# Mixers' loads on GpSimd's queue, a staging buffer of its own for the modulation, and split weights in four places of 128 columns

## The chip, the core and the metric

The kernel runs on one core of a Trainium2 chip. The metric is the device time of one execution in microseconds, the median of several runs. The core has a tensor engine for matrix products (PE), a vector engine (DVE), a scalar engine for activations (ACT), a general engine (GpSimd, called POOL in the profile) and an engine that only synchronises and starts transfers (SP). Each engine works through its own list of instructions in order. Transfers (DMAs) are started by an instruction in the list of SP, ACT or POOL: such an instruction waits for its semaphores there, and all that stands behind it in that list waits with it.

## What is computed

A model of two layers works on two streams of tokens, the latent `l` (512 tokens) and the context `c` (256 tokens), with 1024 channels, in float32:

```python
for i in range(DEPTH):                       # 2 layers
    m_l = split(silu(c)     @ mod_w[i] + mod_b[i], 6)   # modulation: shift, scale, gate, twice
    m_c = split(silu(c_ctx) @ mod_w[i] + mod_b[i], 6)
    ul = split_cols(modulate(rms_norm(h_l), m_l[0], m_l[1]) @ w_in[i])   # 1024 x 2696
    uc = split_cols(modulate(rms_norm(h_c), m_c[0], m_c[1]) @ w_in[i])
    y_l = concat(ssd(ul, uc), hyena(ul), retention(ul, uc), s5(ul, uc)) @ w_out[i]
    h_l = h_l + m_l[2] * y_l
    h_l = h_l + m_l[5] * swiglu(modulate(rms_norm(h_l), m_l[3], m_l[4]), w_up[i], w_down[i])
    ...                                      # the same for the context, in the first layer alone
return rms_norm(h_l)
```

Four mixers share the columns of the input projection: SSD (a scan with 4 heads), Hyena (long convolutions by spectra, whose filters are made by a small network), retention (a scan with 4 heads and a rotary table) and S5 (a complex diagonal state space with 16 groups).

## The kernel before

**Products.** A float32 matrix product is made of three products of float32r parts (`mm3`, matmuls at L126). A weight comes as pieces of 128 columns by 1024 rows (512 KB): `piece` (L207) loads one into the staging tile `wst`, which has three buffers, on SP's queue; `split` makes the high part `whi` on ACT (L155) and the low part `wlo` on DVE (L134); `weights` collects two pieces into one pair of tiles `whi`, `wlo` of 256 columns, of which there are two in turn (pool `whl`, two buffers each). `held` (L227) does the same for the output projection's second half. `dt_weights` takes a whole pair for 128 columns (`wd`, L1125), and block `sb` a pair for one piece.

**Modulation of the first layer.** `mod` makes 256 columns at a time: two loads of 512 KB (each four of the eight row tiles) through the same `wst` buffers, 16 matmuls `wst,csil` with 32 rows of output into one PSUM bank (ring `md`, one bank), a copy by ACT (`mrow`), two small matmuls `const,mrow` and an addition on DVE (`modv`). Eight such blocks stand in `start`, twelve more among blocks 5 to 10 of the input projection (`in_proj`). The second layer's modulation and a last eighth of the first's are products on DVE (`mod_vec`, L361, loads `mvw` on POOL's queue).

**Order of the work.** A scheduler writes each engine's list at build time from priorities (`at`, `flow`) and a simulated timeline. The big projections carry `bulk` (their priority is pushed back by 300000), so that the mixers' small products go first and the projections fill in. PSUM banks come from rings: `mm` (3 banks) for the projections, `xb` (2) and `xa` (2) for the mixers, `md` (1). In the first layer ring `xb` makes the Hyena filters of the context and of the latent stream (`sirens`, `filters`), then the convolutions of the context, then those of the latent stream; ring `xa` makes the S5 blocks (`s5_mats` with `s5_block`, eight blocks of two groups), then `s5_out`, then SSD; retention follows in `mm` and `xa`. The output projection begins after them.

**Small loads of the mixers.** Before, SP's list holds besides the weights: the rotary table (L1645), in the first layer the filters' small weights and tables (L504 to L540: `w`, `feat`, `win`) and their spectra's stores (L598: `F0`), the SSD's and retention's decay rows (`E` L897, `CE` L964, `scanm` L1156), and S5's rotations (`s5rot` L1466), kernels (`KT` L1471, read from what ACT's queue wrote as `s5k`), inputs (`s5U` L1473) and the loads of `s5_out` (`s5fu` L1535, `s5fy` L1537), and the mixers' outputs that are read back (`yl` L1714). POOL's list holds the filters' Fourier tables (`ftab`, L581), in the second layer all that the filters load, and some element-wise work (`fam`, `aloc`, `alol`, `t`, and the mask on `E`, L719).

Of the kernel before, what the change touches and what calls it, by code (L numbers as in the profile page):

```python
# [17 lines left out]
D = 1024  # L18
# [88 lines left out]
class Kern:  # L107
# [7 lines left out]
    def at(self, p):  # L115
        """Instructions in this block get priorities from p on."""
# [44 lines left out]
    def pst(self):  # L161
        """A PSUM bank from the ring of the current flow of work."""
# [13 lines left out]
    def flow(self, fl, p=None):  # L176
        """Work that takes its banks and small tiles from rings of its own; p: its priority."""
# [10 lines left out]
    def rsq(self, v, n):  # L188
        """v: (128, n) tile, replaced by 1/sqrt(v)."""
# [13 lines left out]
    def piece(self, src, nk, ncol):  # L203
        """src: (128, nk * ncol) of a weight laid out by pieces."""
        pool, tag = self.stage
        st = pool.tile([128, 1024], F32, tag=tag, name="wst", bufs=2 if tag == "stw" else 3)[:, :nk * ncol]
        self.nc.sync.dma_start(st, src)  # L207
        return st.rearrange("p (k n) -> p k n", k=nk)

    def weights(self, srcs, nk=8):  # L210
        """Pieces of 128 columns as high and low parts."""
        hi = self.whl.tile([128, 8, 256], F32R, tag="wh", name="whi")
        lo = self.whl.tile([128, 8, 256], F32R, tag="wl", name="wlo")
        for h, src in enumerate(srcs):
            cs = slice(128 * h, 128 * h + 128)
            self.split(hi[:, :nk, cs], lo[:, :nk, cs], self.piece(src, nk, 128))
        return hi, lo

    def held(self, src):
        """Four tiles of rows of a weight with all its columns, src: (8, 128, 512)."""  # L220
        W = []
        for m0 in (0, 4):
            hi = self.whl.tile([128, 8, 256], F32R, tag="wh", name="whi").rearrange("p k n -> p (k n)")
            lo = self.whl.tile([128, 8, 256], F32R, tag="wl", name="wlo").rearrange("p k n -> p (k n)")
            for h in range(2):
                st = self.wst.tile([128, 1024], F32, tag="st", name="wst")
                self.nc.sync.dma_start(st.rearrange("p (m x) -> p m x", m=2),  # L227
                                       src[m0 + 2 * h:m0 + 2 * h + 2].rearrange("m p x -> p m x"))
                self.split(hi[:, 1024 * h:1024 * h + 1024], lo[:, 1024 * h:1024 * h + 1024], st)
            W += [[t[:, 512 * m:512 * m + 512].rearrange("p (k n) -> p k n", k=4) for t in (hi, lo)] for m in range(4)]  # L230
        return W

    def proj(self, ps, W, c0, m, a, nk=8, order=None):
        hi, lo = W
        ah, al = a
        with self.bulk():
            for q, k in enumerate(order or range(nk)):
                self.mm3(ps, hi[:, k, c0:c0 + m], lo[:, k, c0:c0 + m], ah[k], al[k], q == 0, q == nk - 1)
# [14 lines left out]
    def run(self):  # L253
        nc, tc, A = self.nc, self.tc, self.A
        es = ExitStack()
        with es:
# [4 lines left out]
            self.whl = ec(tc.tile_pool(name="whl", bufs=2))  # L261
# [15 lines left out]
    def put_y(self, s, k, t, c0=0):  # L277
        """Keep tile k of the mixers' output: as operands of the output projection where these have room already."""
# [12 lines left out]
    def ytiles(self, s, p):  # L291
        """Tiles that are not written in the order of their making: each has its own place."""
# [41 lines left out]
    def mod(self, i, c0, c1):  # L334
        """Columns 256*c0 .. 256*c1 of the modulation of layer i."""
        for cc in range(c0, c1):
            with self.flow("md"):
                ps = self.pst()
            for h in range(2):
# [3 lines left out]
            r = self.tile_t(self.sc, "mrow")  # L343
            self.act(r, ps[:, :256])
            p2 = ps[:, 256:260]
            for h in range(2):
                self.mm(p2[:, 2 * h:2 * h + 2], r[:, 128 * h:128 * h + 128], self.sel[:, 3:5])
            self.add(self.modv[i][:, 2 * cc:2 * cc + 2, :], p2.rearrange("p (a b) -> p a b", a=2),
                     self.vec[i][:, 2 * cc:2 * cc + 2][:, :, None].to_broadcast([128, 2, 2]))
# [20 lines left out]
    def gains(self, i, part, s, gat):  # L370
        """(1 + scale) * g for a stream; part is 1 or 4."""
# [1531 lines left out]
```

## Time and profile before

| what | us |
|---|---|
| median of three runs | 1916.04 (1914.66 to 1916.39) |
| span of the profiled execution | 1919.5 |
| PE busy in it | 1790.1 |
| DVE busy | 1257.5 |
| ACT busy | 713.5 |
| POOL busy | 207.3 |

The profiled execution's own time is its span, 1919.5 us, from the first instruction to the last; it lies 3.5 us above the median of the runs. Busy times are of instructions that compute; the issue of transfers from SP isn't counted. The mean granted clock of PE was 0.960 of its full 2.4 GHz. In the page's slices the clock reads full in most of the span, and lower where PE had gaps: in the first layer's mixers (0 to 520 us), in the second layer's (1180 to 1560) and at the end.

### The profile page before, as it was taken

To read this page: it belongs to the slowest core of one execution; us is meant where nothing else is said; L and a number is where in the kernel's file an instruction comes from. 1 tells how busy PE (TensorE), PEld (TensorE's weight loads), DVE (VectorE), ACT (ScalarE), POOL (GpSimd) and SP (SyncE) were. 2 spreads that over 40 slices of the span, in tenths; PEclk is the share of its full clock that TensorE was granted. 3 is DMA by queue.
4 is the path that set the end of the run, shared out by engine and by line. 5 is a ranking of instruction groups with operands and counts; after the bars stand their busy time and mean duration, and the time that the engine had idled before them with its cause. 6 is when DMAs were issued, how large, how long until landed. Compare 5 with 4: busy or idle time off the path is not lost.

```text
span 1919.5 us, 28992 instructions
## 1 busy us (share of the span) xinstructions
PE 1790.1 (93%) x10792; PEld 1526.3 (80%) x10792; DVE 1257.5 (66%) x2941; ACT 713.5 (37%) x1390; POOL 207.3 (11%) x273
## 2 busy tenths in 40 slices
PE   3789878898999999999999999989999999999997
PEld 2678767686789888888888989878866888888886
DVE  8788764778858899777665427678576843233336
ACT  4354234555227223212132115514673542222222
POOL 0201121123002000011223000121110000000000
PEclk9899979998899999999999999999997999999998
DMA  6656588765612335656635513565563322222331
GB/s 231 178 138 186 149 180 229 243 192 160 203 56 89 121 123 164 219 190 230 210 113 131 155 44 123 158 207 159 153 201 96 126 73 94 89 96 88 97 101 56
DMA packets 193089, 280.87 MB, mean 146 GB/s; under 512 B 51745, under 2 KB 127837, under 8 KB 192436
## 3 DMA queue, kind: packets, MB, share of 16 engines
q1 hardware_dynamic: 107188, 166.20, 28.5%
q10 hardware_dynamic: 55920, 64.72, 10.9%
q0 software_dynamic: 29840, 48.09, 8.9%
q8 instruction: 85, 1.39, 0.3%
q14 instruction: 56, 0.46, 0.1%
HBM read 235.00 MB, written 43.96 MB: 145 GB/s over the span
## 4 chain that ended last, share of the span: by engine, by line
PE 58%; DVE 11%; issue 8%; DMA 8%; ACT 3%; POOL 1%; ACTq 0%; SPq 0%; DVEq 0%; POOLq 0%
PE ps_mm L126 31%; PE ps_xb L126 20%; PE ps_xa L126 4%; DMA mvw<-in_wmt_dram 4%; PE ps_md L126 2%; DMA wst<-in_wi_dram 1%; ACT L155 1%; DVE mvo L364 1%; DVE wlo L134 1%; DVE gt L134 1%; DVE t L134 1%; DVE g L1499 1%; DVE cst L134 1%; DVE s5tmp L134 1%; ACT whi L155 1%
## 5 line engine op out<-in xcount | busy, mean ns | idle before, releaser
L155 ACT ACTIVATE whi<-wst 128x1024 fp32r<-128x1024 f32 (+3 forms) x226 | 198.9, 917 | 361.5 <-PE ps_mm L126 169.4
L134 DVE TENSOR_TENSOR wlo<-wst,whi 128x1024 fp32r<-128x1024 f32 (+3 forms) x226 | 233.9, 1058 | 83.5 <-ACT whi L155 81.2
L126 PE MATMUL ps_mm<-alol,whi 128*128 128x512 f32 (+1 forms) x688 | 262.7, 383 | 0.4 <-POOL alol L134 0.4
L126 PE MATMUL ps_mm<-ahl,wlo 128*128 128x512 f32 (+1 forms) x688 | 262.3, 382 | 0.0
L126 PE MATMUL ps_mm<-ahl,whi 128*128 128x512 f32 (+1 forms) x688 | 260.9, 383 | 0.3 <-ACT ahl L155 0.2
L126 PE MATMUL ps_mm<-h,whi 128*128 128x512 f32 (+1 forms) x592 | 168.8, 365 | 0.9 <-DVE h L134 0.7
L126 PE MATMUL ps_xb<-ahl,whi 128*128 128x512 f32 (+1 forms) x416 | 154.2, 373 | 3.8 <-ACT ahl L155 3.8
L126 PE MATMUL ps_xb<-ahl,wlo 128*128 128x512 f32 (+1 forms) x416 | 153.8, 370 | 0.0
L126 PE MATMUL ps_xb<-alol,whi 128*128 128x512 f32 (+1 forms) x416 | 153.5, 371 | 0.1
L134 DVE TENSOR_TENSOR sg<-sg,ps_mm 128x512 f32<-128x512 f32 (+1 forms) x70 | 39.9, 570 | 172.9 <-PE ps_mm L126 172.7
L126 PEld LDWEIGHTS ps_mm<-alol,whi 128*128 128x128 f32 x688 | 130.7, 190 | 26.4 <-issue 2.7
L126 PEld LDWEIGHTS ps_mm<-ahl,wlo 128*128 128x128 f32 x688 | 130.7, 190 | 24.5 <-issue 1.1
L126 PEld LDWEIGHTS ps_mm<-ahl,whi 128*128 128x128 f32 x688 | 130.2, 191 | 25.0 <-issue 1.6
L126 PE MATMUL ps_xb<-h,whi 128*128 128x256 f32 (+1 forms) x592 | 129.2, 310 | 0.1
L364 DVE SCALAR_TENSOR_TENSOR mvo<-mvw,crow 128x1024 f32<-128x1024 f32 x80 | 97.8, 1222 | 39.6 <-DMA mvw<-in_wmt_dram 38.7
L126 PE MATMUL ps_mm<-ahc,whi 128*128 128x256 f32 x368 | 107.4, 296 | 13.0 <-ACT whi L155 8.6
L126 PEld LDWEIGHTS ps_mm<-h,whi 128*128 128x128 f32 x592 | 103.7, 188 | 17.5 <-DVE h L134 1.2
L126 PE MATMUL ps_mm<-aloc,whi 128*128 128x256 f32 x368 | 108.2, 295 | 1.0 <-DVE aloc L134 1.0
L126 PE MATMUL ps_mm<-ahc,wlo 128*128 128x256 f32 x368 | 107.1, 293 | 2.0 <-DVE wlo L134 2.0
L126 PEld LDWEIGHTS ps_xb<-h,whi 128*128 128x128 f32 x592 | 98.9, 188 | 11.6 <-issue 1.1
L126 PE MATMUL ps_mm<-h,wlo 128*128 128x512 f32 (+1 forms) x296 | 107.9, 365 | 0.0
L155 ACT ACTIVATE h<-sg 128x512 fp32r<-128x512 f32 (+1 forms) x70 | 37.4, 534 | 161.7 <-DVE sg L134 161.6
(576 smaller groups left out, 4137.3 us busy)
## 6 DMA issues: line engine op xcount, KB each, us to landing
wst<-in_wu_dram SPq DMA_DIRECT2D x88, 512.0 KB
mvw<-in_wmt_dram POOLq DMA_DIRECT2D x56, 512.0 KB, 3.7
wst<-in_wi_dram SPq DMA_DIRECT2D x42, 512.0 KB
wst<-in_wm_dram SPq DMA_DIRECT2D x40, 512.0 KB
wst<-in_wd_dram SPq DMA_DIRECT2D x24, 384.0 KB
ftab<-in_c_ftL_dram POOLq DMA_DIRECT2D x32, 256.0 KB, 5.0
wst<-in_wd_dram SPq DMA_DIRECT2D x32, 256.0 KB
s5rot<-s5r SPq DMA_DIRECT2D x32, 192.0 KB
```

The lines of the kernel that those rows point to most:

```text
L126: return self.nc.tensor.matmul(out, lhsT, rhs, start=start, stop=stop)
L134: return (eng or self.nc.vector).tensor_tensor(out, a, b, op=op)
L155: return self.nc.scalar.activation(out, in_, func, bias=bias, scale=scale)
L364: self.nc.vector.scalar_tensor_tensor(o, st, 1.0, crow[:, q], op0=ALU.mult, op1=ALU.mult, accum_out=mv[:, c, q:q + 1])
L1499: nc.vector.tensor_tensor_scan(o, dcy, x, 0.0, ALU.mult, ALU.add)
```

## The change

Three things change together.

1. The mixers' loads and stores that stood in SP's list are put into POOL's list (`nc.gpsimd.dma_start` in place of `nc.sync.dma_start`): some 190 DMAs. SP's list then holds the inputs, all weights with their modulation, and half of the output.
2. The modulation is made 128 columns at a time, 40 blocks instead of 20, each with one load of 512 KB (all eight row tiles) and 8 matmuls of 128 columns. Its loads have a staging tile of their own, `mst`, with one buffer; `wst` has two buffers instead of three. In `start` the loads take `wst`, `mst`, `wst` in turn, and the PSUM banks come from rings `md` and `mm` in turn; in `in_proj` only `mst` and `md` are used.
3. The weights' parts lie in one tile `WH` and one tile `WL` of four places of 128 columns, which are taken in a ring (`slot`). A pair of pieces takes two places as before, `wd` and block `sb` take one each.

```diff
-    def piece(self, src, nk, ncol):
-        pool, tag = self.stage
-        st = pool.tile([128, 1024], F32, tag=tag, name="wst", bufs=2 if tag == "stw" else 3)[:, :nk * ncol]
+    STAGE = dict(st=2, stw=2, mst=1)
+    def piece(self, src, nk, ncol, ring=None):
+        pool, tag = (self.wst, ring) if ring else self.stage
+        st = pool.tile([128, 1024], F32, tag=tag, name="mst" if ring else "wst", bufs=self.STAGE[tag])[:, :nk * ncol]
         self.nc.sync.dma_start(st, src)
         return st.rearrange("p (k n) -> p k n", k=nk)
+    def slot(self, n=1):
+        at = self.nslot % 4
+        if at + n > 4:
+            at, self.nslot = 0, self.nslot + 4 - at
+        self.nslot += n
+        return at
     def weights(self, srcs, nk=8):
-        hi = self.whl.tile([128, 8, 256], F32R, tag="wh", name="whi")
-        lo = self.whl.tile([128, 8, 256], F32R, tag="wl", name="wlo")
+        at = self.slot(len(srcs))
         for h, src in enumerate(srcs):
-            cs = slice(128 * h, 128 * h + 128)
-            self.split(hi[:, :nk, cs], lo[:, :nk, cs], self.piece(src, nk, 128))
-        return hi, lo
+            self.split(self.WH[:, at + h, :nk], self.WL[:, at + h, :nk], self.piece(src, nk, 128))
+        return [t[:, at:at + len(srcs)] for t in (self.WH, self.WL)]
...
-    def mod(self, i, c0, c1):
-        for cc in range(c0, c1):
-            with self.flow("md"):
+    def mod(self, i, c0, c1, fl="md", rings=("mst",)):
+        for c in range(c0, c1):
+            st = self.piece(self.A["wm"][i, c], 8, 128, rings[c % len(rings)])
+            with self.flow(fl):
                 ps = self.pst()
-            for h in range(2):
-                st = self.piece(self.A["wm"][i, cc][:, 1024 * h:1024 * h + 1024], 4, 256)
-                for g in range(4):
-                    self.mm(ps[32 * g:32 * g + 32, :256], self.csil[:, 4 * h + g, :], st[:, g], h == 0, h == 1)
+            for k in range(8):
+                g = 32 * (k % 4)
+                self.mm(ps[g:g + 32, :128], self.csil[:, k, :], st[:, k], k < 4, k >= 4)
...
         for j in range(4):
-            self.mod(0, j, j + 1)
-            self.mod(0, 4 + j, 5 + j)
+            for c in (2 * j, 8 + 2 * j):
+                self.mod(0, c, c + 2, "md+mm", ("st", "mst", "st"))
...
-                    self.mod(0, 2 * q - 2, 2 * q)
+                    self.mod(0, 4 * q - 4, 4 * q)
...
-        dma = (nc.gpsimd if i else nc.sync).dma_start
+        dma = nc.gpsimd.dma_start
...
-        wd = self.wd = self.whl.tile([128, 8, 256], F32R, tag="wh", name="wd")[:, :, 0:128]
+        wd = self.wd = self.WH[:, self.slot()]
...
-            nc.sync.dma_start(rot[64 * h:64 * h + 64], rd[b].rearrange("(r n) x -> n r x", r=2))
+            nc.gpsimd.dma_start(rot[64 * h:64 * h + 64], rd[b].rearrange("(r n) x -> n r x", r=2))
...
-            nc.sync.dma_start(KT[:, g], bass.AP(tensor=kd.tensor, offset=kd.offset + (g0 + g) * 8 * 3840 + 112,
+            nc.gpsimd.dma_start(KT[:, g], bass.AP(tensor=kd.tensor, offset=kd.offset + (g0 + g) * 8 * 3840 + 112,
...
```

**SP's list.** Before, this stood in SP's list while the first layer's S5 blocks and filters run (`in_wi` is the input projection, `in_wm` the modulation):

```order
L207 DMA wst<-in_wi_dram 128x1024
L1156 DMA scanm<-in_c_scan_dram 64x512
L1123 DMA dtw<-in_wi_dram 128x64
L1471 DMA KT<-s5k_1632 128x1x128 x2
L1466 DMA s5rot<-s5r_332 64x2x384 x2
L207 DMA wst<-in_wi_dram 128x1024 x2
L536 DMA w_1197<-in_hy_w_dram 128x2x256
L1471 DMA KT<-s5k_1632 128x1x128
L1473 DMA s5U<-s5u_427 128x1x128 x2
L1471 DMA KT<-s5k_1632 128x1x128
L207 DMA wst<-in_wi_dram 128x1024
```

After the change SP's list reads from about the same weight on (`in_wo` is the output projection):

```order
L209 DMA wst<-in_wi_dram 128x1024 x3
L1130 DMA dtw<-in_wi_dram 128x64
L209 DMA wst<-in_wi_dram 128x1024 x11
L209 DMA mst<-in_wm_dram 128x1024 x5
L209 DMA wst<-in_wi_dram 128x1024
L209 DMA mst<-in_wm_dram 128x1024 x2
L209 DMA wst<-in_wi_dram 128x1024
L209 DMA mst<-in_wm_dram 128x1024 x5
L209 DMA wst<-in_wo_dram 128x512 x3
```

Eleven pieces of the input projection follow one another there, with nothing of the mixers between them; the modulation's loads come behind most of them.

**POOL's list.** Before, from the start's last `aloc`, `alol` on, POOL's list reads (`ftab` are the Fourier tables, `fam` a product in the filters):

```order
L581 DMA ftab<-in_c_ftC_dram 128x2x128 x4
L134 TENSOR_TENSOR aloc<-nt,ahc 128x256
L134 TENSOR_TENSOR alol<-nt,ahl 128x512
L1125 MEMSET wd 128x8x128
L134 TENSOR_TENSOR fam<-fam 128x512
L581 DMA ftab<-in_c_ftC_dram 128x2x128 x4
L134 TENSOR_TENSOR fam<-fam 128x512
L581 DMA ftab<-in_c_ftL_dram 128x4x128 x4
L134 TENSOR_TENSOR fam<-fam 128x512 x3
```

After the change S5's loads stand among the filters' loads and `fam` there:

```order
L543 DMA w_1209<-in_hy_w_dram 128x2x256
L588 DMA ftab<-in_c_ftC_dram 128x2x128 x4
L1132 MEMSET whi 128x1024
L1480 DMA s5U<-s5u_429 128x1x128 x4
L547 DMA win<-in_c_winC_dram 128x512 x2
L1163 DMA scanm<-in_c_scan_dram 64x512
L1478 DMA KT<-s5k_1726 128x1x128 x2
L1473 DMA s5rot<-s5r_334 64x2x384 x2
L1478 DMA KT<-s5k_1726 128x1x128
L1480 DMA s5U<-s5u_429 128x1x128 x2
L1478 DMA KT<-s5k_1726 128x1x128
L1473 DMA s5rot<-s5r_334 64x2x384 x2
```

The lists of 260 (SP) and 112 (POOL) entries have become lists of 71 and 267.

**PE's list.** In PE's list after the change, in the part of the second stream's filters, blocks of the modulation stand like this (`ps_md` is the one bank of ring `md`, `w,fh` a product of the filters, `s5fy,glw` one of `s5_out`):

```order
L126 MATMUL ps_xb<-w_1547,fh 128x256 x2
L126 MATMUL ps_md<-mst,csil 32x128 x8
L126 MATMUL ps_md<-const,mrow 128x2
L126 MATMUL ps_md<-mst,csil 32x128 x8
L126 MATMUL ps_md<-const,mrow 128x2
L126 MATMUL ps_xa<-s5fy,glw 128x256
L126 MATMUL ps_md<-mst,csil 32x128 x8
L126 MATMUL ps_md<-const,mrow 128x2
L126 MATMUL ps_xb<-w_1547,fh 128x256 x2
```

Three blocks, each of which reads a fresh load of the one buffer `mst`, follow one another with one other product between them. Before, the blocks there are of 256 columns with two loads each, and stand among the projection's products.

**DVE's list.** Before, DVE's first `hw` (the first filter weighted by its window, from bank `xb`) is the list's entry 365 and stands behind this:

```order
L134 TENSOR_TENSOR wlo<-wst,whi 128x8x128
L134 TENSOR_TENSOR W<-early,s5BC 128x256 x2
L134 TENSOR_TENSOR gt<-gt,s5sg 128x384
L134 TENSOR_TENSOR wlo<-wst,whi 128x8x128
L134 TENSOR_TENSOR Kf<-Kf,ps_xa 16x16
L134 TENSOR_TENSOR gt<-ps_xa,s5rot 128x384
L134 TENSOR_TENSOR W<-W,s5tmp 128x256
L152 SCALAR_TENSOR_TENSOR dt<-dt,dt_2492 64x512
L134 TENSOR_TENSOR hw<-ps_xb,win 128x512
```

After the change it is entry 409, behind this:

```order
L152 SCALAR_TENSOR_TENSOR sx<-ps_mm,vec,sx 128x255
L1506 SCALAR_TENSOR_TENSOR g_1866<-dec_100,gt 128x96 x4
L134 TENSOR_TENSOR W<-W,s5tmp 128x256
L134 TENSOR_TENSOR gt<-g_1866,s5rot 128x384
L152 SCALAR_TENSOR_TENSOR s5sg<-g_1866,s5rot 64x384
L134 TENSOR_TENSOR s5sg<-g_1866,s5rot 64x384
L134 TENSOR_TENSOR s5tmp<-early,s5BC 128x288
L134 TENSOR_TENSOR gt<-gt,s5sg 128x384
L134 TENSOR_TENSOR wlo<-wst,whi 128x1024
L134 TENSOR_TENSOR s5M<-s5M,s5tmp 128x288
L152 SCALAR_TENSOR_TENSOR sx<-ps_mm,vec,sx 128x511
L134 TENSOR_TENSOR hw<-ps_xb,win 128x512
```

44 entries more of S5, of weights and of the projection's epilogues (`sx`) stand ahead of the first filter's window.

## Rows read from the trace of the kernel before

**Rows 1.** Page, section 1: busy time and share of the span by engine.

```profile
PE 1790.1 (93%) x10792; PEld 1526.3 (80%) x10792; DVE 1257.5 (66%) x2941; ACT 713.5 (37%) x1390; POOL 207.3 (11%) x273
```

**Rows 2.** Windows by stage: length, busy us, granted clock, DMA share, GB/s.

```profile
core 0: us, PE busy (x) PEld busy (x) DVE busy (x) ACT busy (x) POOL busy (x), PEclk, DMA share, GB/s
...
60.00:280.00 220.00, 191.83 (x1216) 159.63 (x1216) 174.84 (x406) 87.32 (x181) 35.70 (x39) 0.90 0.63 164
280.00:440.00 160.00, 143.45 (x1021) 119.59 (x1020) 100.25 (x203) 80.21 (x168) 31.51 (x32) 0.96 0.76 219
440.00:520.00 80.00, 69.78 (x451) 55.67 (x450) 67.48 (x177) 35.36 (x80) 14.57 (x20) 0.83 0.57 184
520.00:1180.00 660.00, 656.81 (x4083) 579.15 (x4081) 452.14 (x1067) 195.13 (x388) 74.16 (x115) 1.00 0.46 140
1180.00:1560.00 380.00, 354.84 (x2282) 310.85 (x2282) 275.28 (x620) 198.20 (x394) 47.53 (x59) 0.93 0.50 151
1560.00:1880.00 320.00, 320.00 (x1373) 257.53 (x1373) 110.38 (x125) 79.37 (x102) 0.00 (x0) 1.00 0.29 93
```

**Rows 3.** Chain that ended last, 280 to 440: start, length, what.

```profile
284.13 7.47 DMA wst<-in_wi_dram
...
335.44 4.89 DMA wst<-in_wi_dram
...
369.48 4.06 DMA wst<-in_wi_dram
...
397.15 7.60 DMA wst<-in_wi_dram
...
434.75 5.72 DMA wst<-in_wo_dram
```

**Rows 4.** Waits of SP's queue, 0 to 520: us in total, times, longest.

```profile
SPq L207 <- PE ps_md L126: 115.7, 22, 17.6
SPq L207 <- DVE wlo L134: 39.3, 14, 8.0
SPq L1471 <- DMA s5k<-Kf: 39.1, 14, 5.7
```

**Rows 5.** Waits of PE, 60 to 520.

```profile
PE ps_md L126 <- DMA KT<-s5k: 9.7, 3, 5.6
PE ps_mm L126 <- ACT whi L155: 8.6, 1, 8.6
```

**Rows 6.** Windows of 40 us, columns as in the second group.

```profile
240.00:280.00 40.00, 32.89 (x207) 26.48 (x206) 30.48 (x66) 12.86 (x29) 9.18 (x11) 0.74 0.70 168
280.00:320.00 40.00, 31.45 (x204) 27.22 (x203) 16.41 (x32) 17.27 (x28) 3.80 (x6) 0.91 0.99 247
320.00:360.00 40.00, 34.11 (x228) 26.98 (x227) 23.90 (x45) 28.04 (x62) 9.11 (x9) 0.91 0.70 202
```

**Rows 7.** PE's timeline in the start: start, length, operation, idle before.

```profile
54.88 1.07 PE L126 MATMUL ps_md<-wst,csil 128*32 128x256 f32 x16 [0.27 <-DVE modv L134]
...
64.58 1.94 PE L126 MATMUL ps_md<-wst,csil 128*32 128x256 f32 x16 [3.57 <-DVE modv L134]
```

**Rows 8.** Page, section 6: a load from POOL, KB each, us to landing.

```profile
mvw<-in_wmt_dram POOLq DMA_DIRECT2D x56, 512.0 KB, 3.7
```

**Rows 9.** Instructions of line 581: duration in ns minimum, median, maximum; first, last start.

```profile
L581 POOL DMA_DIRECT2D ftab<-in_c_ftL_dram x32: 740/750/785, 185.0 to 1049.0; - x32
```

**Rows 10.** Instructions of tile KT, 100 to 300.

```profile
L1471 SPq DMA_DIRECT2D KT<-s5k x16: 572/584/614, 116.6 to 259.0; - x16
```

**Rows 11.** Instructions of tile hw, 100 to 300.

```profile
L134 DVE TENSOR_TENSOR hw<-ps_xb,win x12: 670/691/692, 133.8 to 267.6; 128x512 f32<-128x512 f32 x12
```

**Rows 12.** Waits of POOL, 0 to 600.

```profile
POOL fam L134 <- ACT fam L155: 82.9, 8, 31.9
...
POOL E L719 <- ACT sdec L155: 56.0, 6, 20.6
POOL t L134 <- DVE vm L134: 54.8, 3, 27.4
```

More of the change, by code (lines that the diff above doesn't have):

```diff
@@ L217, in weights @@
-        return hi, lo
+            self.split(self.WH[:, at + h, :nk], self.WL[:, at + h, :nk], self.piece(src, nk, 128))
+        return [t[:, at:at + len(srcs)] for t in (self.WH, self.WL)]
     def held(self, src):
         W = []
-        for m0 in (0, 4):
-            hi = self.whl.tile([128, 8, 256], F32R, tag="wh", name="whi").rearrange("p k n -> p (k n)")
-            lo = self.whl.tile([128, 8, 256], F32R, tag="wl", name="wlo").rearrange("p k n -> p (k n)")
-            for h in range(2):
[L226 to L230, printed above, removed]
@@ L231, in held @@
-        return W
-    def proj(self, ps, W, c0, m, a, nk=8, order=None):
-        hi, lo = W
+        for m in range(0, 8, 2):
+            at = self.slot()
+            hi, lo = [t[:, at].rearrange("p k n -> p (k n)") for t in (self.WH, self.WL)]
+            st = self.wst.tile([128, 1024], F32, tag="st", name="wst", bufs=2)
+            self.nc.sync.dma_start(st.rearrange("p (m x) -> p m x", m=2), src[m:m + 2].rearrange("m p x -> p m x"))
+            self.split(hi, lo, st)
+            W += [[t[:, 512 * j:512 * j + 512].rearrange("p (o k n) -> p o k n", o=1, k=4) for t in (hi, lo)] for j in range(2)]
@@ L235, in proj @@
+        return W
+    def proj(self, ps, W, c0, a, nk=8, order=None):
+        hi, lo = [t[:, c0 // 128] for t in W]
         ah, al = a
@@ L260, in run @@
             self.wst = ec(tc.tile_pool(name="wst", bufs=3))
-            self.whl = ec(tc.tile_pool(name="whl", bufs=2))
+            self.whl = ec(tc.tile_pool(name="whl", bufs=1))
+            self.WH = self.whl.tile([128, 4, 8, 128], F32R, name="whi")
+            self.WL = self.whl.tile([128, 4, 8, 128], F32R, name="wlo")
+            self.nslot = 0
             self.ps = ec(tc.tile_pool(name="ps", bufs=2, space=PSUM))
@@ L332, in load_x @@
                 nc.sync.dma_start(tiles[k], self.A["x" + s.name][:, k])
-    def mod(self, i, c0, c1):
-        for cc in range(c0, c1):
-            with self.flow("md"):
+    def mod(self, i, c0, c1, fl="md", rings=("mst",)):
+        for c in range(c0, c1):
+            st = self.piece(self.A["wm"][i, c], 8, 128, rings[c % len(rings)])
+            with self.flow(fl):
                 ps = self.pst()
-            for h in range(2):
-                st = self.piece(self.A["wm"][i, cc][:, 1024 * h:1024 * h + 1024], 4, 256)
-                for g in range(4):
-                    self.mm(ps[32 * g:32 * g + 32, :256], self.csil[:, 4 * h + g, :], st[:, g], h == 0, h == 1)
[L343 to L349, printed above, removed]
+            for k in range(8):
+                g = 32 * (k % 4)
+                self.mm(ps[g:g + 32, :128], self.csil[:, k, :], st[:, k], k < 4, k >= 4)
+            r = self.tile_t(self.sc, "mrow")[:, :128]
+            self.act(r, ps[:, :128])
+            p2 = ps[:, 256:258]
+            self.mm(p2, r, self.sel[:, 3:5])
+            self.add(self.modv[i][:, c, :], p2, self.vec[i][:, c:c + 1].to_broadcast([128, 2]))
     def mod_vec(self, i, cols, both, p):
@@ L500, in sirens @@
     def sirens(self, i, streams, p):
[L502 removed]
+        dma = self.nc.gpsimd.dma_start
         w1 = p.tile([33, 64], F32, name="w1")
@@ L1060, in in_h @@
             ps = self.pst()
-            self.proj(ps[:, :n], W, 128 * c, 128, s.a)
+            self.proj(ps[:, :n], W, 128 * c, s.a)
             tl = 2 * g + c
@@ L1102, in in_r @@
             ps = self.pst()
-            self.proj(ps[:, :n], W, 128 * c, 128, s.a)
+            self.proj(ps[:, :n], W, 128 * c, s.a)
             t = self.tile_t(s, "r" + which)
@@ L1172, in ssd_in @@
         ps = self.pst()
-        self.proj(ps[:, :n], W, 0, 128, s.a)
+        self.proj(ps[:, :n], W, 0, s.a)
         self.conv3(BC, ps[:, :n], i, 64, 3, 2, 73, n)
@@ L1189, in s5_in @@
             for c in range(2):
-                self.proj(pp[c][:, c0:c1], W, 128 * c, 128, [[t[:, c0:c1] for t in h] for h in s.a])
+                self.proj(pp[c][:, c0:c1], W, 128 * c, [[t[:, c0:c1] for t in h] for h in s.a])
         for c in range(2):
@@ L1723, in body @@
                     ps = self.pst2("mm+mm+md")[:, :s.L]
-                    self.proj(ps, W, 128 * (m % 2), 128, [[h[k] for k in KA] for h in ya[s.name]], nA)
+                    self.proj(ps, W, 128 * (m % 2), [[h[k] for k in KA] for h in ya[s.name]], nA)
                     xo = self.tile_t(s, "xo")
@@ L1736, in body @@
                     ps = self.pst2()[:, :c1 - c0]
-                    self.proj(ps, WB[m], 0, 128, [[h[k][:, cs] for k in KB] for h in ya[s.name]], 8 - nA)
+                    self.proj(ps, WB[m], 0, [[h[k][:, cs] for k in KB] for h in ya[s.name]], 8 - nA)
                     x = nx[s.name][m][:, cs]
@@ L1794, in body @@
                                 ps = self.pst2()[:, :c1 - c0]
-                                self.proj(ps, W, 0 if fin else 128 * (m % 2), 128, [[t[:, cs] for t in h] for h in H[s.name]], nf)
+                                self.proj(ps, W, 0 if fin else 128 * (m % 2), [[t[:, cs] for t in h] for h in H[s.name]], nf)
                                 x = self.x[s.name][m][:, cs]
```

39 lines of the change are left out of this document (19 added, 20 removed).

## The prediction

> **What bounds the kernel now.** I read the page's busy line first, then windows by stage, then the chain that ended last, then the waits of SP's queue, of PE and of POOL where the windows showed idle PE. PE is busy for 1790.1 of 1919.5 us and DVE for 1257.5 [rows 1], so at most some 130 us can be had without taking work from PE. The windows say where they lie [rows 2]: PE idles 28.2 us between 60 and 280, 16.6 between 280 and 440, 10.2 between 440 and 520 (55 us in the first layer's mixers), 3.2 in the 660 us of the first layer's second half, 25.2 between 1180 and 1560 (the second layer's mixers), and nothing in the 320 us after it. The rest (some 47 us) is the start and the end. The clock goes with it: 1.00 where PE has no gaps, 0.90 and 0.83 in the first layer's mixers.
>
> In the stretch 280 to 440 the chain goes five times through a transfer of a weight, for 7.47, 4.89, 4.06, 7.60 and 5.72 us, 29.7 together [rows 3]. These weights are not late for lack of buffers alone: SP's queue, which starts them, stands still before an instruction that waits for others. Up to 520 us it waited 115.7 us for the modulation's matmuls to free a staging buffer, 39.3 for `wlo`, and 39.1 for S5's kernels to reach DRAM before it may load `KT` [rows 4]; each weight behind such an instruction is started late. PE itself shows one wait for a weight's high part, 8.6 us, and three for `KT`, 9.7 [rows 5]. When the weights are late, DVE has nothing to do either: in 280 to 360 it is busy for 16.4 and 23.9 of 80 us, and DMA's share is 0.99 in the first half of that [rows 6].
>
> **The change, part by part.** The sum is made against the profiled span, 1919.5 us, which lies 3.5 us above the median; the forecast takes these 3.5 us off at the end. A difference under 0.2%, some 3.8 us, is what a measurement here can't tell from none.
>
> *Weights no longer behind the mixers in SP's list.* Eleven pieces of the input projection stand in a row in SP's new list, and the `KT` waits are gone from it. The projection's products run 22 to 25 us of PE work further ahead of the mixers' in PE's list than before (counted in the lists, with each matmul at its columns' time at full clock). The gain has two bounds: the one wait that PE shows, 8.6 us [rows 5], and all five pieces of the chain, 29.7 [rows 3]. I take the middle, -19, since a late weight that is no longer late uncovers part of the next wait: next late are then the filters' and S5's own results.
>
> *Start.* The modulation's blocks there had one bank in turn with DVE's addition: the block at 54.88 and the next at 64.58 stand 9.7 us apart, and the second waited 3.57 for `modv` [rows 7]. With two banks in turn this wait can go; DVE is the other limit there, so the gain is 0 to -10 and I take -4, one such wait.
>
> *Clock.* The same 16 matmuls took 1.07 us at full clock and 1.94 after a pause [rows 7]. A granted 0.74 over 240 to 280 [rows 6] means some 21 us at the lower level (1.2 instead of 2.4 GHz), and 0.83 over 440 to 520 [rows 2] some 27; half of both would be lost, 24 us, had PE been busy throughout. It wasn't, and new pauses are made elsewhere: I take -5, between 0 and -12.
>
> *One buffer for the modulation.* A load of 512 KB can start only when the last matmul of the block before has read `mst`. Most of the 24 blocks in the projection have several us of products between them. Two intervals have nearly none (the three blocks in a row in PE's list in the section on the change), and four others less than a load. A load of the same size from POOL lands in 3.7 us [rows 8], one on the chain in 4.1 to 7.6 [rows 3]. Two full loads and a little of the four make +8; 0 if the mixers' waits cover them, +20 at the longest of both rows. While PE stands at such a block, all of the mixers' products behind it stand too, which is why it counts in full. The 20 more copies, small products and additions of the split blocks lie beside other work: PE's two 128-column products have the columns of one of 256.
>
> *Places of 128 columns.* `wd` and `sb` take a place each instead of a pair. That is worth a split (about 2 us) or two in the projection and is in the first term. In the feed-forward network nothing changes but the third staging buffer. There 1373 matmuls fill 320 us without idle [rows 2], 0.233 us each; a piece's 24 products of 512 columns last 5.6 us, longer than a load's 3.7 [rows 8]. I take 0, at most +5 where a piece of fewer rows is used up faster.
>
> *The mixers' loads in POOL's list.* The issues themselves: a Fourier table in 512 pieces holds POOL for 0.740 to 0.785 us [rows 9], a `KT` load held SP for 0.584 [rows 10]. Some 190 issues at 0.75 make 143 us on an engine that is busy for 207 of 1919 [rows 1]; in 60 to 280 some 75 of them, 56 us, come to the 35.7 there [rows 2]. POOL isn't full, and 0.17 us more for an issue is 0 off the path, at most +5 for the 32 `KT` and `s5U` loads of the first layer's S5 blocks, should all stand in its chain.
>
> Order is what can cost. POOL works its list in order, and it already waited 82.9 us for `fam`'s operand, 56.0 for `E`'s and 54.8 for `t`'s up to 600 us [rows 12]. Behind these now stand S5's `KT`, `s5rot` and `s5U`, the filters' `win` and tables, the stores of `F0`, and later `E` and `CE`; who waits for them are PE's products of S5 and DVE's `hw`. Besides, the new lists put the mixers later on DVE: the first `hw`, at 133.8 us before [rows 11], has 44 entries more ahead of it. At the mean of the stage, 174.84 us in 406 instructions [rows 2], these are 19 us; with each operation's own mean I count 24. The stage 280 to 360 had 39.7 us of idle DVE [rows 6], which was idle because weights were late, so most of these 24 us can be made up there. I take +8, a third; bounds 0 and +24.
>
> *The second layer.* Its S5 and SSD loads go to POOL as well; PE's 25.2 us of idle there [rows 2] come from results of DVE and ACT more than from weights. 0, between -8 and +15.
>
> Sum: -19 - 4 - 5 + 8 + 8 + 0 = -12, so 1907.5 for a profiled span and, less 3.5, 1904 us. Its own range is 1894 to 1910.
>
> **A rule weighed.** Table loads that POOL issued between 185 and 1049 us took 0.740 to 0.785 us each, all 32 of them [rows 9], while DVE was busy for some 70 to 80% of those stages [rows 2]: a DMA's issue there didn't stretch beside DVE's work. The Trainium skill, in "SBUF — State Buffer", section "SBUF: two separate sides", says that descriptors of transfers from GpSimd can't be written while DVE runs an operation in its two-port mode, so that a transfer of 0.62 us alone took about 3.1 us beside a copy. By that rule 190 loads would each be late by some 2.5 us and the mixers' chain by tens of us. The rows speak against it for this kernel's operations.
>
> **Rivals.**
>
> *Mixers late on POOL (slower).* The place is the first layer's filters and S5: a load of `win` or `KT` stands behind a `fam` that waits for ACT, S5 and the filters hold each other up, and DVE's 24 us aren't made up. Then the weights' gain falls to its lower bound, since PE would wait for the mixers instead: -8.6 - 4 - 5 + 8 + 24 = +14, 1930 us. The sign turns when the mixers' term passes +20 with the rest as taken, and at +10 with the weights at 8.6. For it: the 82.9, 56.0 and 54.8 us that POOL waited in order [rows 12]. Against it: those waits are mostly idle ones whose operands come when the mixer needs them anyway.
>
> *More of the idle time goes.* If the weights' five pieces all go (-29.7), the clock gives -10 and the modulation costs +5, with the start's -4 and the mixers' +8, the sum is -31, 1885 us. For it: 55 us of idle PE [rows 2], and all four causes in SP's list go at once. Against it: DVE's 67.5 of 80 us in 440 to 520 [rows 2], where it is near its own limit.
>
> *Nothing is left.* The weights were late because the 16 DMA engines were full (0.99 in 280 to 320 [rows 6]), not because SP stood; or the one buffer `mst` costs +20, since SP's weights stand behind its loads. In the first case weights 0, start -4, clock 0, modulation +4 and mixers 0 make 0; in the second -19 - 4 - 5 + 20 + 8 makes 0 too: 1916 us, between 1912 and 1920. The Trainium skill, in "DMA: Bandwidth & Descriptors", section "Issuing engines are not separate DMA queues", holds for the first of these: all queues run on the same 16 engines, and a second issuing engine saves issue time only. Against it stand SP's 115.7, 39.3 and 39.1 us of waiting [rows 4], which are order and no bandwidth, and a share of 0.76 over 280 to 440 [rows 2].
>
> *DVE holds up POOL's transfers.* 20 of the loads on the mixers' chain late by 1 us each make the sum +8, 1924 us. The constant issue times [rows 9] speak against it.
>
> **How the numbers follow.** The forecast .42 (1894 to 1910); more of the idle time .13 (1878 to 1894); nothing left .16 (1912 to 1920); mixers late .25 (1920 to 1940); POOL's transfers held up .04. Faster by over 0.2% is .42 + .13 = .55; the same .16; slower .25 + .04 = .29. The range leaves out the outer part of the gain's case and of the mixers' case, some .05 and .13: 1882 to 1928.
>
> **What the profile would show.** Right: the five weight transfers gone from the chain in 280 to 440, SP's waits for `KT` gone and its waits for `ps_md` now before `mst`; PE's idle 60 to 520 near 40 us instead of 55; the first `hw` at 140 to 160 us but the filters' end no later than before. Wrong: PE waits for `win`, `KT` or `fam` that rise above 20 us, PE waits for `in_wm` above 20 us at the modulation's blocks, or POOL's issues above 1 us. The prediction fails first in the mixers' term: whether POOL's order delays them by more than 20 us can't be read from the trace of before.

## The result and the profile after

The changed kernel takes 1960.69 us (median of 4 runs, 1955.63 to 1965.63) against 1915.35 for the kernel before (4 runs): 1.0242 times as long, 95% interval 1.0216 to 1.0267, some 46 us slower. The forecast was 1904 us, the range ended at 1928.

The page's busy line of the changed kernel, which answers to [rows 1]:

```profile
span 1962.8 us, 29751 instructions
...
PE 1806.4 (92%) x11112; PEld 1542.7 (79%) x11112; DVE 1264.3 (64%) x2961; ACT 717.5 (37%) x1405; POOL 342.8 (17%) x490
```

No engine has much more to compute: DVE and ACT are busy for 7 and 4 us longer, and of PE's 16 us more some 8 are in the modulation's blocks (640 matmuls of 128 columns for 320 of 256), the others the same products at a lower mean clock (0.942 for 0.960). POOL's 135 us more are the issues of 217 transfers; these were moved, not some 190. The rest is waiting. Windows by stage of the changed kernel, with the columns of [rows 2]:

```profile
60.00:280.00 220.00, 198.21 (x1346) 168.60 (x1338) 173.19 (x402) 85.38 (x178) 82.05 (x119) 0.93 0.66 173
280.00:440.00 160.00, 134.24 (x1007) 110.71 (x1008) 90.73 (x199) 83.47 (x172) 50.59 (x60) 0.89 0.64 196
440.00:520.00 80.00, 65.36 (x448) 50.77 (x447) 62.87 (x159) 28.38 (x75) 25.86 (x35) 0.70 0.37 109
...
1200.00:1600.00 400.00, 360.90 (x2313) 314.62 (x2313) 278.62 (x638) 193.19 (x391) 95.48 (x136) 0.91 0.48 143
```

From 60 to 280 us PE idles less than before, 21.8 us for 28.2. Then it turns: 25.8 us of idle for 16.6, 14.6 for 10.2, at a granted clock of 0.70 for 0.83 in the last of these. The second layer begins 27 us late and its mixers lose 17 more: 39 us of idle in 1200 to 1600 where there were 25 in 1180 to 1560 [rows 2]. The transfers in the chain that ended last say what became of the weights; they are all that stand there between 264 and 460 us (start, length, what), and answer to [rows 3]:

```profile
269.06 10.53 DMA s5fy<-s5y
279.87 6.18 DMA win<-in_c_winL_dram
312.04 6.46 DMA s5fu<-s5u
327.61 3.46 DMA s5fy<-s5y
340.58 6.56 DMA E<-acd0c
405.35 6.77 DMA hin<-dhy0l
429.47 6.97 DMA E<-acd0l
445.71 5.86 DMA E<-acd0l
```

No weight stands in the chain any more, as forecast, and in the place of five weights (29.7 us) and one `s5fu` (9.05 us, at 271.46) stand seven loads that now come from POOL's list (46.0 us) and one, `hin`, from ACT's. POOL's timeline at the first two shows what stands ahead of them (start, length, operation, idle before and its releaser):

```profile
263.23 3.00 POOL L588 DMA_DIRECT2D ftab<-in_c_ftL_dram  x4 [4.79 <-PE ps_xb L126]
266.18 1.47 POOL L605 DMA_DIRECT2D F0l<-fo  x2
267.61 0.60 POOL L1536 DMA_DIRECT2D glw<-in_glu_dram  x1
268.16 0.91 POOL L1542 DMA_DIRECT2D s5fu<-s5u  x1
269.06 0.88 POOL L1544 DMA_DIRECT2D s5fy<-s5y  x1
273.62 0.88 POOL L1544 DMA_DIRECT2D s5fy<-s5y  x1 [3.68 <-DMA ftab<-in_c_ftL_dram]
275.00 0.88 POOL L904 DMA_DIRECT2D E<-acd0c  x1 [0.50 <-DMA ftab<-in_c_ftL_dram]
275.87 0.69 POOL L948 MEMSET Hn<- 64x256 f32 x2
276.51 2.47 POOL L971 DMA_DIRECT2D CE<-acd0c  x4
278.97 0.56 POOL L547 DMA_DIRECT2D win<-in_c_winL_dram  x1
279.87 0.55 POOL L547 DMA_DIRECT2D win<-in_c_winL_dram  x1 [0.34 <-DMA s5fy<-s5y]
```

The filters' window `win` stands behind the issues of nine loads of S5 and SSD, and one of these waits 3.68 us. DVE's `hw`, which reads it, is late: its first start moved from 133.8 [rows 11] to 153.2 us, its last from 267.6 to 302.0:

```profile
L134 DVE TENSOR_TENSOR hw<-ps_xb,win x12: 672/686/692, 153.2 to 302.0; 128x512 f32<-128x512 f32 x12
```

But `win` itself is not what holds it up: up to 320 us DVE waits 1.1 us for it, once. What DVE waits for ahead of the last four `hw` stands in its list before them:

```profile
268.89 0.16 DVE L134 TENSOR_TENSOR modv<-ps_md,vec 128x2 f32<-128x2 f32 x1 [3.08 <-PE ps_md L126]
275.08 0.16 DVE L134 TENSOR_TENSOR modv<-ps_md,vec 128x2 f32<-128x2 f32 x1 [6.03 <-PE ps_md L126]
279.66 0.48 DVE L152 SCALAR_TENSOR_TENSOR s5fy<-s5fu,vec,s5fy 128x256 f32<-128x256 f32 x1 [4.42 <-DMA s5fy<-s5y]
285.01 0.16 DVE L134 TENSOR_TENSOR modv<-ps_md,vec 128x2 f32<-128x2 f32 x1 [4.86 <-PE ps_md L126]
288.50 0.99 DVE L134 TENSOR_TENSOR CE<-CE,sin 128x512 f32<-128x512 f32 x1 [3.33 <-ACT CE L155]
```

Three additions of the modulation, `modv`, stand between the eighth and the ninth `hw` in DVE's new list, where none stood before, and two of them wait for PE at blocks whose `mst` is late (PE's two waits below). With the same lists and the mixers' loads back on SP (the seventh run below) `hw` runs from 149.2 to 293.7 us, so of the 34 us at its end some 8 go with POOL's queue.

SP's waits up to 520 us answer to [rows 4]; the waits for `s5k` have left SP's list (POOL has them, 48.6 us, 13 times), but SP isn't free of waits:

```profile
SPq L209 <- DVE wlo L134: 122.7, 15, 20.4
SPq L209 <- PE ps_md L126: 108.0, 27, 10.8
SPq L209 <- DMA mst<-in_wm_dram: 94.6, 22, 8.3
```

PE's two waits at the modulation's blocks that stand in a row:

```profile
272.99 1.08 PE L126 MATMUL ps_md<-mst,csil 128*32 128x128 f32 x16 [2.50 <-DMA mst<-in_wm_dram]
282.92 1.08 PE L126 MATMUL ps_md<-mst,csil 128*32 128x128 f32 x16 [7.88 <-DMA mst<-in_wm_dram]
```

In the start PE waits for the modulation's loads too. Up to 530 us before, and up to 580 after (us in total, times, longest):

```profile
PE ps_md L126 <- DMA wst<-in_wm_dram: 15.3, 5, 7.4
...
PE ps_mm L126 <- DMA mst<-in_wm_dram: 19.6, 4, 8.7
PE ps_md L126 <- DMA mst<-in_wm_dram: 14.2, 4, 7.9
```

Of these 33.8 us, 23.3 fall in the first 60 us, where all of the 15.3 before fall, and 10.5 behind them.

### The profile page after: what moved, and what is told of

Its sections match the earlier page's. It is cut to its first block, busy times and chain, and to the rows that moved or that the text cites. A ratio compares the mean times of both kernels' runs of the same rounds, so it can differ in the third digit from the quotient of the medians.

```text
span 1962.8 us, 29751 instructions
## 1 busy us (share of the span) xinstructions
PE 1806.4 (92%) x11112; PEld 1542.7 (79%) x11112; DVE 1264.3 (64%) x2961; ACT 717.5 (37%) x1405; POOL 342.8 (17%) x490
## 4 chain that ended last, share of the span: by engine, by line
PE 55%; DMA 11%; DVE 9%; issue 7%; ACT 3%; POOL 2%; ACTq 0%; DVEq 0%; POOLq 0%
PE ps_mm L126 27%; PE ps_xb L126 21%; PE ps_xa L126 5%; DMA mvw<-in_wmt_dram 4%; PE ps_md L126 2%; DMA E<-acd1l 1%; DVE mvo L371 1%; ACT L155 1%; DMA s5fy<-s5y 1%; DVE wlo L134 1%; DMA wst<-in_wu_dram 1%; DMA E<-acd0l 1%; DMA s5fu<-s5u 1%; DVE t L134 1%; ACT whi L155 0%
## 5 line engine op out<-in xcount | busy, mean ns | idle before, releaser
L155 ACT ACTIVATE whi<-wst 128x1024 fp32r<-128x1024 f32 (+3 forms) x226 | 207.8, 922 | 538.4 <-PE ps_mm L126 209.3
L134 DVE TENSOR_TENSOR wlo<-wst,whi 128x1024 fp32r<-128x1024 f32 (+3 forms) x226 | 238.1, 1056 | 194.6 <-ACT whi L155 191.9
L126 PE MATMUL ps_mm<-ahl,whi 128*128 128x512 f32 (+1 forms) x704 | 268.6, 385 | 6.3 <-ACT ahl L155 1.3
L126 PE MATMUL ps_mm<-alol,whi 128*128 128x512 f32 (+1 forms) x704 | 270.5, 385 | 0.3 <-POOL alol L134 0.3
L126 PE MATMUL ps_xb<-ahl,wlo 128*128 128x512 f32 (+1 forms) x416 | 153.2, 369 | 0.0
L126 PE MATMUL ps_mm<-ahc,whi 128*128 128x256 f32 x384 | 109.8, 291 | 10.8 <-ACT ahc L155 8.3
L126 PEld LDWEIGHTS ps_xb<-ahl,whi 128*128 128x128 f32 x416 | 79.4, 192 | 16.2 <-ACT ahl L155 3.3
```

What stands on the lines that cost most here:

```text
L126: return self.nc.tensor.matmul(out, lhsT, rhs, start=start, stop=stop)
L134: return (eng or self.nc.vector).tensor_tensor(out, a, b, op=op)
L155: return self.nc.scalar.activation(out, in_, func, bias=bias, scale=scale)
```

## The experiments

All ratios are to the kernel before, run on the same chip; us are the ratio times 1916. Theory A: the mixers' loads are late in POOL's list. Rival B: the modulation's one buffer. Rival C: the edits make the scheduler write other lists for PE, DVE and ACT, and these cost.

**The parts alone.** First POOL's queue alone, in before:

```diff
-            nc.sync.dma_start(KT[:, g], ...
+            nc.gpsimd.dma_start(KT[:, g], ...
...
```

> The kernel before with the mixers' loads in POOL's list and nothing else of the change. Theory A (POOL's order delays the mixers, and that is the loss): 30 to 50 us slower than before, the first hw later than 150 us, the last hw later than 290, the second layer's S5 blocks from 13 to 14.5 us each. Rival B (the modulation's single buffer is the loss): within 10 us of before. Rival C (the four places and the new order of the lists): within 10 us of before.

1950.88 us, 1.0164 (1.0133 to 1.0195): 31 us slower. The time is theory A's, its signs are not: the first `hw` starts at 136.2 us, not after 150, and the last at 283.5, not after 290. Then the converse, the changed kernel with these loads back on SP (the same lines turned round):

> The changed kernel with the mixers' loads back in SP's list; the modulation's staging and the four places stay. Theory A: within 10 us of before, some 40 us faster than the changed kernel. Rival B: 25 to 45 us slower than before, as the changed kernel is. Rival C: 25 to 45 us slower than before.

1937.27 us, 1.0094 (1.0062 to 1.0126): 18 us slower than before. The loads are not the whole loss. The modulation alone (`mod`, `mst`, two `wst` buffers in before):

> The kernel before with the modulation by 128 columns, its one staging buffer and two buffers for the weights; pairs of 256 columns and loads on SP stay. Theory A: between 5 us faster and 12 us slower (two waits for mst of some 10 us together). Rival B: 25 to 45 us slower. Rival C: within 5 us.

1936.06 us, 1.0084 (1.0052 to 1.0117): 16 us, more than A (12) and C (5) had, less than B. B as the whole cause falls. The four places alone (`slot`, `WH`, `WL` in before):

> The kernel before with the four places of 128 columns only; modulation, three staging buffers and loads on SP as before. Theory A and rival B: within 5 us of before. Rival C: 20 us slower or more.

1954.48 us, 1.018 (1.0153 to 1.0207): 34 us, where two theories had nothing. Each part costs, and the sums don't fit: places and modulation together cost 18, not 50. That speaks for C, and asks for runs in which the lists are held.

**Lists held.** Kernel before and the first run are made of the same instructions; only the queue of some differs. So the lists of PE, DVE and ACT can be pinned, instruction by instruction, to those of another kernel, with SP's and POOL's left to the scheduler:

```diff
         Kern(tc, A, out).run()
+        pinned(tc, nc)   # each instruction of a list after the one before it
```

Loads on POOL, lists of before:

> The kernel before with the mixers' loads in POOL's list, while the lists of PE, DVE and ACT are pinned word for word to those of before; only SP's and POOL's lists are new. Theory A (the loads are late behind others in POOL's list): 25 to 40 us slower than before, as with the scheduler's own lists (31). Theory C (the scheduler, told of the new queue, wrote other lists for PE, DVE and ACT, and these cost): within 8 us of before.

1960.88 us, 1.0212 (1.0185 to 1.0238): 41 us. A holds here. SP's list is new too, but the weights in it are not later: ACT waits 14.9 us for `wst<-in_wi` between 100 and 560 us, where it waited 15.6. Loads on SP, lists that were written for loads on POOL:

> The converse: the kernel before with all loads on SP as before, and the lists of PE, DVE and ACT pinned to those that the scheduler wrote with the loads on POOL. Theory A: within 8 us of before. Theory C: 25 to 40 us slower than before.

1951.35 us, 1.0178 (1.0158 to 1.0199): 34 us, with no load moved. C holds as well. The same crossing for the changed kernel; first its own lists with loads on SP:

> The changed kernel with the mixers' loads back on SP, but with the changed kernel's own lists of PE, DVE and ACT. Theory A: near the run with loads back on SP and its own lists, 10 to 25 us slower than before. Theory C: near the changed kernel, 38 to 50 us slower than before.

1946.19 us, 1.0143 (1.0116 to 1.017): 27 us. And its loads on POOL with the lists that were written for loads on SP:

> The changed kernel, its loads on POOL, with the lists of PE, DVE and ACT that the scheduler wrote when the loads were back on SP. Theory A: 38 to 50 us slower than before, as the changed kernel. Theory C: 10 to 25 us slower than before, as with the loads on SP.

1969.14 us, 1.0259 (1.0238 to 1.028): 50 us. So the queue alone, with the lists held, costs 41 and 32 us in lists written for SP (the fifth run against before, this one against the second), 19 in the changed kernel's (1.0242 less 1.0143), and -3 in those of the first run (1.0164 less 1.0178, inside the intervals): lists that were written for POOL's queue hide much or all of its price, and cost themselves: 34 us in the kernel before, and in the changed kernel 27 where lists written for SP cost 18.

With equal lists the n-th product of PE is the same in both, and the difference of its starts shows where the fifth run falls behind (starts in before and in this run, us, and the difference):

```
first filter product   101.8    106.2    4.5
s5U,KT                 258.1    269.0   10.8
projection             340.1    355.9   15.8
projection             404.1    421.3   17.2
output projection      520.2    545.4   25.2
second layer, begin   1180.2   1204.0   23.8
second layer          1260.2   1287.8   27.6
second layer          1320.1   1352.7   32.6
second layer          1420.0   1459.2   39.2
end                   1900.1   1939.1   39.0
```

No one place: no single product adds more than 3.1 us, and most of those that add over 1 are of S5, the filters, SSD and retention. (The control below that has these lists and costs nothing drifts by up to 5.5 us against before in the same comparison, so the first row is not clear of that.) DVE's and ACT's waits for loads between 100 and 560 us that grew, first before:

```profile
DVE hw L134 <- DMA win<-in_c_winL_dram: 4.9, 2, 3.3
DVE s5fy L152 <- DMA s5fy<-s5y: 3.0, 1, 3.0
...
ACT yhc L155 <- DMA yl<-yd0c: 4.3, 2, 2.9
```

and with the loads on POOL in the same lists:

```profile
DVE hw L134 <- DMA win<-in_c_winL_dram: 9.8, 3, 4.6
DVE s5fy L152 <- DMA s5fy<-s5y: 8.8, 2, 5.0
DVE hw L134 <- DMA win<-in_c_winC_dram: 2.6, 1, 2.6
...
ACT sdec L155 <- DMA E<-acd0l: 8.8, 4, 5.5
ACT yhc L155 <- DMA yl<-yd0c: 7.9, 2, 5.0
```

**Group by group**, in the lists of before (the same edit as the fifth run, for some of the lines):

> The kernel before with PE's, DVE's and ACT's lists pinned to its own, and only the S5 blocks' loads (s5ML, s5rot, KT, s5U) in POOL's list. Theory A1 (each load lands later from POOL, by its longer issue and landing): the four groups add up to the 41 us that all loads cost in these lists; this one 12 to 20 us slower. Theory A2 (the groups stand in each other's way in one list; alone, none does): under 6 us slower, the four together under 20.

1927.28 us, 1.0049 (1.0034 to 1.0064): 9 us.

> The same with only the first layer's filter loads and stores (w, feat, win, F0) in POOL's list. A1: 5 to 10 us slower. A2: within 4 us.

1923.23 us, 1.0028 (1.0008 to 1.0047): 5 us.

> The same with only the decay rows of SSD (E, CE, scanm) and two small tables in POOL's list. A1: 8 to 14 us slower, since an E issue took 0.9 us and landed after 6 to 9 from POOL. A2: within 5 us.

1936.55 us, 1.009 (1.0069 to 1.0111): 17 us.

> The same with only the loads of s5_out (glw, s5fu, s5fy), of the mixers' outputs (yl) and the rotary table in POOL's list. A1: 6 to 12 us slower. A2: within 4 us.

1921.82 us, 1.0015 (0.9997 to 1.0033): 3 us, not clear of none. The four make 35 of the 41 us, so most of the price is there when a group is alone in POOL's list with POOL's own work. The 6 us left for one mixer standing in another's way are not clear of none, as each run's interval is 3 to 5 us to either side. The dearest group shows how. `E` in before (duration in ns minimum, median, maximum; first, last start):

```profile
L897 SPq DMA_DIRECT2D E<-acd0l x4: 377/380/483, 388.5 to 444.1; - x4
```

and with SSD's loads on POOL:

```profile
L897 POOL DMA_DIRECT2D E<-acd0l x4: 910/934/953, 396.3 to 452.9; - x4
...
DMA to landing us min/median/max: 6.3/6.9/11.3
```

An issue takes 0.93 us for 0.38. The last of the four started 8.8 us later than before, where PE was some 5 us late. Before, it started 1.4 us after POOL began to mask the `E` ahead of it (442.71 us); here 5.3 us after, since it stands behind the `t` products that POOL computes:

```profile
447.59 1.22 POOL L719 TENSOR_SCALAR_AFFINE_SELECT E<-E 128x512 f32<-128x512 f32 x2 [7.80 <-ACT sdec L155]
448.78 2.66 POOL L134 TENSOR_TENSOR t<-vp,Ft 128x512 f32<-128x512 f32 x1
451.52 1.41 POOL L134 TENSOR_TENSOR t<-t,t 128x256 f32<-128x256 f32 x2
452.87 0.93 POOL L897 DMA_DIRECT2D E<-acd0l  x1
```

The longer issues can't be all of it. Over all 217 transfers of the fifth run, each with its median issue on POOL less that on SP, they come to 29 us, and that would be their price only if every one stood on the path. By the medians at least some 12 of the 41 us have another source: order, or a later landing (SP's transfers show none in the trace), or PE's lower granted clock (0.954 for 0.960 over the span).

**What a new set of lists costs.** The places again, with two places for `sb` and `wd`, so that these take what a pair took (only `held` still takes single places):

```diff
-        at = self.slot(len(srcs))
+        at = self.slot(2)
...
-        wd = self.wd = self.WH[:, self.slot()]
+        wd = self.wd = self.WH[:, self.slot(2)]
```

> The kernel before with the four places, of which block sb and wd take two each, so that every weight takes what a pair took before; loads and modulation as before. Theory C1 (the block sx, which can come earlier with the places, is what puts the mixers later): within 6 us of before, since sb and wd hold two places again. Theory C2 (any new set of lists costs, whatever it was made for): 10 to 35 us slower.

1941.53 us, 1.0111 (1.0074 to 1.0148): 21 us; the looser hold of `sb` and `wd` isn't needed for a loss. Two controls that move no load; the first should be neutral, the second also changes which buffers the second block's small tiles take:

```diff
-        st = self.sm.tile([128, 8, 8], F32, tag="dtw", name="dtw", bufs=1)
+        st = self.sm.tile([128, 8, 8], F32, tag="dtw", name="dtw", bufs=2)
```

> A neutral control: before, with two buffers instead of one for a tile of 256 bytes (dtw), which moves some 1600 lines of PE's list and 520 of DVE's and changes no load, bank or place. C1: within 4 us of before. C2: 8 us slower or more.

1935.84 us, 1.0094 (1.0057 to 1.0131): 18 us, for a second buffer that nothing needed.

```diff
-        self.one_ring = q < 2
+        self.one_ring = q < 1
```

> A second neutral control: before, with the second block of columns in the ring of small tiles that the later blocks use; it moves some 4400 lines of PE's list. C1: within 5 us of before. C2: 10 us slower or more, more than the first control.

1930.72 us, 1.0078 (1.0048 to 1.0107): 15 us, though it moves more of PE's list than the first; it was not run with its lists held. The first control with its lists held to those of before:

> The first neutral control (two buffers for dtw) with the lists of PE, DVE and ACT pinned to those of before. If the new lists were its whole cost: within 4 us of before. If the edit itself costs: 12 to 20 us slower, as with its own lists.

1919.41 us, 0.9995 (0.9977 to 1.0014): nothing. All of that control's cost was its lists. Its windows with its own lists show the place, the end of the first layer's mixers:

```profile
280.00:440.00 160.00, 136.60 (x930) 113.50 (x928) 92.83 (x191) 76.62 (x161) 30.44 (x31) 0.93 0.72 208
440.00:520.00 80.00, 62.29 (x394) 48.06 (x393) 53.23 (x144) 31.30 (x72) 15.83 (x20) 0.78 0.45 133
```

PE works 198.9 us there, 213.2 in before [rows 2], and the clock is lower. Before with the places' list of PE, DVE's and ACT's lists written anew around it:

> The kernel before, pairs of 256 columns and all, with PE's list pinned to the one that the scheduler wrote for the four places. C2, and the new order as the cause of the places' 34 us: 20 to 40 us slower. If the places themselves cost (weights that wait for a place): within 10 us of before.

1999.81 us, 1.0422 (1.0383 to 1.0461): 81 us, more than either theory had. A list of PE made for other hold times makes its own waits, so this run shows that an order can cost that much, not what the places' order costs with the places.

**One group taken back in the changed kernel**, its lists held:

> The changed kernel with its own lists of PE, DVE and ACT, and of its loads only SSD's decay rows (E, CE, scanm) and two small tables back on SP. By the price of that group in the lists of before (17 us): 10 to 17 us faster than the changed kernel, 28 to 36 slower than before. If the loads cost by standing in each other's way: more than 20 us faster, or under 6.

1962.31 us, 1.0225 (1.0185 to 1.0264), where the changed kernel had 1.0242: 3 us, not clear of none, and not 17. A group's price in the lists of before doesn't carry over to lists that were written with that load on POOL.

No run was faster than the kernel before.

## Why the prediction was wrong

**The sum held a wrong term and lacked one.** The step that failed first is "I take +8, a third; bounds 0 and +24" for the mixers' loads in POOL's list. With the lists of before it measured +41, in the changed kernel's own lists +19. The +8 was sized from DVE's list alone: 24 us of entries ahead of the first `hw`, of which two thirds would be made up. The lateness of the loads themselves got no price. In the fifth run DVE's list is that of before, and the 41 us are there all the same.

The rival "mixers late on POOL" had the sign and the place, and 1930 us; its price was the same 24 us of DVE's entries. Two things stood against a price for the loads. One is "those waits are mostly idle ones whose operands come when the mixer needs them anyway", which SSD's last `E` answers with some 4 us behind POOL's `t` products. The other is "0.17 us more for an issue is 0 off the path". That excess was taken from `KT` (0.584 on SP [rows 10]; 0.614 from POOL, hardly more), and not from `E`, whose issue more than doubled; and DVE's and ACT's longer waits for `win`, `s5fy`, `E` and `yl` show loads on the path. How the 41 us divide between order and issue is not known beyond that: the issues can be 29 at most.

**The missing term: new lists.** The prediction read the new lists for places that get better or worse and priced those. It had no price for a new set of lists as such. Two small edits cost 18 and 15 us, and the first of them nothing once its lists were held. The changed kernel costs 27 us in its own lists with every load on SP, against the forecast's sum of -12 for all of the change. So of the changed kernel's 46 us 19 go with POOL's queue, and 27 with its lists, the modulation and the places together. Whether the modulation (16 alone) and the places (34 alone, 21 as pairs) cost anything beyond new lists was not settled: their instructions are not those of before, or could not be put in that order.

**Weights, -19: the wait went, the gain didn't come.** The five transfers left the chain, and the projection ran ahead (21.8 us of idle up to 280 for 28.2). But what was "next late" took the place of all of it: the mixers' loads, and the modulation's blocks on PE and DVE. With the lists of before, taking the mixers' loads from SP's list shortened one wait of PE for `whi` by 3.8 us.

**Start, -4:** wrong in sign; the first filter product came at 106.6 us for 101.8, with the loads on POOL or not (107.2 and 104.7 in the second and third run): some -4 became +3 to +5. The wait that the term took did shrink (PE for `modv`, 4.5 us to 1.2 up to 100 us), but PE waited 23.3 us for the modulation's loads there in place of 15.3, which the term had left as they were. **One buffer, +8:** right for the blocks in the projection, where the waits are 10.5 us, nearly all of it the two in the row. It left out the start's 8 us more. **Clock, -5:** wrong in sign, as PE had more gaps: 0.70 for 0.83 in 440 to 520. **Second layer, 0 (-8 to +15):** +17. Both causes reach it: with the lists of before the loads make it 15 us longer (the fifth run), and without a load moved the lists for POOL's queue make it 22 us longer (the sixth), the changed kernel's own 8 (the seventh). **First `hw` at 140 to 160 us:** 153.2; "the filters' end no later than before" was wrong by 34 us, of which some 8 go with POOL's queue.

**The rule weighed** was set aside rightly, as far as the issues show. The tables' issues from POOL took 0.740 to 0.810 us with 217 more DMAs in its list (0.740 to 0.785 before [rows 9]), and no issue of a table rose above 1 us. DVE was busy for 57 to 79% of the stages from 60 to 1200 us (63 to 84% before [rows 2], where the prediction reads some 70 to 80). The tables' loads landed after 4.1 us in the middle and 10.1 at most, for 4.8 and 7.0 before; the longest were not followed up. The Trainium skill, "SBUF — State Buffer", section "SBUF: two separate sides", tells of a long hold of transfers from GpSimd while DVE runs an operation in its two-port mode; these issues don't show it. The Trainium skill, "DMA: Bandwidth & Descriptors", section "Issuing engines are not separate DMA queues", says that more issuing engines save issue time only. Here the move did not save even that: from POOL an `E` issue took 0.93 us for 0.38 on SP, and the loads of POOL's list stood behind POOL's own work.

## What to carry to other kernels

Before a scheduled kernel's edit is judged, make a neutral edit and see what a new set of lists costs; here it was 18 us, more than the 12 us of gain that were forecast. Where an edit only moves queues, hold the other engines' lists and compare the same instruction in both traces: the steps of the difference name the loads. Before a load goes to a compute engine's list, ask whether its reader can wait for the operations ahead of it there and for the longer issue; with the lists of before SSD's few rows cost 17 us, S5's many 9.

## What the runs showed of the hardware

The issue of the same transfer takes POOL longer than SP by its shape (medians, before and after): `KT` 0.614 us for 0.584, `s5fy` 0.88 for 0.52, `E` (one row spread over 128 partitions, 512 KB) 0.93 for 0.38. A later landing is not shown: POOL's `E` landed 4.5 to 10.8 us after its issue began (the fifth run), and one that SP issued at 444.07 us was read at 450.12, after its reader had waited for something else, so 6.05 us or less.
